# Attention units of four blocks in four PSUM banks, with transposes in steps of their own

## The chip, the cores and the metric

The kernel runs on one core of one Trainium2 chip. The metric is device time in microseconds (us). TensorE is called PE here, VectorE DVE, ScalarE ACT, GpSimd POOL and SyncE SP, as in the profile.

## The reference

Two layers over x of 1 x 1024 x 1024 in float32, each `x <- x + RMSNorm(mixer(RMSNorm(x)))`. Layer 0 is a gated MLP over chunks of 128 tokens; the change doesn't touch it. Layer 1 is attention, 16 heads of 64, in three groups g with (window, dilation) of (128, 1), (512, 4) and (2048, 16), each with q, k and v of its own:

```python
scores = jnp.einsum('brnihk,brnjhk->brnhij', qb, kk) * scale      # a block of 128 queries, its own keys and the block before
scores = jnp.where(valid, scores, -jnp.inf)                       # causal, at most `steps` back
lse = jax.nn.logsumexp(scores, axis=-1)
o = jnp.einsum('brnhij,brnjhk->brnihk', jnp.exp(scores - lse[..., None]), vv)
...
alpha = jax.nn.softmax(jnp.stack(lses, axis=0), axis=0)           # over the three groups
y = jnp.einsum('gbsh,gbshk->bshk', alpha, jnp.stack(outs, axis=0)) * jax.nn.silu(z)
return y @ w_out
```

## The kernel before

Layer 0 takes the first 735 us or so of the span. What follows is layer 1, and the change lies there.

**Projections.** The normalised rows stand transposed in SBUF, each value as a high and a low part, and a product is three matmuls (`mm3`, L82 to L84: high by high, low by high, high by low). Columns of the weights are cut into 40 chunks: for each q (four heads) and each g one chunk of values (`v_chunk`) and two of queries and keys (`qk_chunk`, pair pr = 0 and 1, two heads each), and one of gates for each q (`z_chunk`). A chunk is seven products (`Chunk.run`, Strassen's scheme), in three banks of PSUM with the tag "mm", and a product is four yields of one `mm3`. `pipeline` strings the products together. What a product leaves is added on DVE (`add`, L87) or copied on ACT, in tiles "u" of `newb`. Queries and keys are rotated on DVE and brought into the tiles Q and K of `qk_tile` by 16 DMAs from SP's queue (L705, L706). POOL and DVE form sums of weights and the low parts (L90), ACT the high parts (L96).

**Attention between them.** `drive` walks over the yields of the pipeline. Each yield is a tick; credit grows by RATE, and whenever it reaches one, `step_side` makes one step of attention, which so lands between two projection matmuls. PE's instructions stay in the order in which the program was written (`manual_schedule`); on the other engines and the queues the planner chooses it, and `high_priority(SOON)` moves what it encloses ahead. `done` of a qk chunk puts the attention of its pair into the queue `side`, to start WAIT = 16 ticks later at the earliest.

A `Unit` holds two heads (hh) and two blocks of 128 queries, or four where g is 2 (`lone`: 128 tokens in each of eight residues, with no block before). `scores` computes into two banks "s", one for each head; DVE adds the mask and takes the row's extreme (L773), ACT takes exp and the sum (L776). `transp` turns the weights by PE into two banks "t" (L798), and ACT copies them to PT (L800). `values` multiplies by V in the one bank "o" (L814); ACT copies it to oT (L819), and SP stores oT in DRAM, in od (L820). `attend` makes one step of three units at once: the transposes of the last, the values of the last but one, and the scores of the new one. `TURN` holds the transposes of V (`turned`, L673).

**Merging.** When the three groups of a pair are through, `merge` is put into `slow`, and `step_slow` makes one of its steps every four ticks: it loads the sums (mg), forms the weights of the three groups, turns them (wT), stores them (wd), and for each half of the tokens loads three results from od (mo, L893 to L897) and their weights (mw, L899), multiplies and adds on DVE, and stores in ybd. The last q's merges and the output product follow the pipeline (`fill`, `ending`).

Of the kernel before, what the change touches and what calls it, by code (L numbers as in the profile page):

```python
# [10 lines left out]
F32 = mybir.dt.float32  # L11
# [11 lines left out]
HD = 64  # L23
RATE = 0.125
WAIT = 16
# [8 lines left out]
def trunk_kernel(  # L34
# [613 lines left out]
    def newb(n):  # L648
        return bp.tile([P, 512], F32, tag="u", bufs=9, name=f"b_{n}")

# [84 lines left out]
    class Unit:  # L735
# [16 lines left out]
        def prev(self, b):  # L752
            return (self.g == 0 and b > 0) or (self.g == 1 and b % 2 == 1)

        def scores(self):

            Qt, Kt = QK[self.q, self.g, self.pr]
            pss = [psum("s", [P, 512], f"s_{self.nm}_{hh}") for hh in range(2)]
            for j, use in enumerate(self.use):
                b, cs = self.b + j, slice(use[0] * P, use[-1] * P + P)  # L760
                for hh in range(2):
                    hs_ = slice(64 * hh, 64 * hh + 64)
                    q_ = block(Qt[hs_, :], self.g, b)
                    k_ = block(Kt[hs_, :], self.g, b, len(use) - 1)
                    nc.tensor.matmul(out=pss[hh][:, cs].rearrange("p (n l) -> p n l", l=k_.shape[2]), lhsT=q_, rhs=k_, start=True, stop=True)  # L765
            self.S = [bp.tile([P, 512], F32, tag="St", bufs=2, name=f"St_{self.nm}_{hh}") for hh in range(2)]
            with tc.high_priority(SOON):
                for j, use in enumerate(self.use):
                    cs = slice(use[0] * P, use[-1] * P + P)
                    mk = mask2 if self.lone else mask[:, use[0] % 2 * P:256]  # L770
                    for hh in range(2):
                        m, z = (self.st[:, self.b + j, hh, i:i + 1] for i in range(2))
                        nc.vector.tensor_tensor_reduce(  # L773
                            out=self.S[hh][:, cs], in0=pss[hh][:, cs], in1=mk, scale=-0.125, scalar=3.0e38,
                            op0=ALU.add, op1=ALU.min, accum_out=m)
# [16 lines left out]
        def transp(self):  # L792
            self.PT = bp.tile([P, 2, 4, P], F32, tag="PT", bufs=2, name=f"PT_{self.nm}")
            pT = [psum("t", [P, 4, P], f"pT_{self.nm}_{hh}") for hh in range(2)]
            for hh in range(2):
                for use in self.use:
                    for k in use:
                        nc.tensor.transpose(out=pT[hh][:, k, :], in_=self.S[hh][:, k * P:k * P + P], identity=ident)  # L798
                with tc.high_priority(SOON):
                    nc.scalar.copy(out=self.PT[:, hh, self.first:], in_=pT[hh][:, self.first:])  # L800

        def values(self):

            V, w = VS[self.q, self.g, self.pr], self.n * P
            po = psum("o", [P, w], f"po_{self.nm}")
            if self.lone:
                todo = [(self.b + j, j, 1, j * P) for j in range(4)]
            else:
                todo = [(self.b, 1, 2, 0), (self.b + 1, 3, 1, P)]
                if self.first == 0:  # L810
                    todo.insert(0, (self.b - 1, 0, 1, 0))
            for n, (kb, k, m, o) in enumerate(todo):
                for hh in range(2):
                    nc.tensor.matmul(  # L814
                        out=po[64 * hh:64 * hh + 64, o:o + m * P], lhsT=V[:, kb, hh, :], rhs=self.PT[:, hh, k:k + m, :].rearrange("p k i -> p (k i)"),
                        start=n == 0, stop=n == len(todo) - 1, skip_group_check=True)
            oT = bp.tile([P, 512], F32, tag="oT", bufs=1, name=f"oT_{self.nm}")[:, 0:w]
            with tc.high_priority(SOON):
                nc.scalar.copy(out=oT, in_=po)  # L819
            nc.sync.dma_start(out=od[self.q][self.pr][self.g][:, self.b * P:self.b * P + w], in_=oT)  # L820
# [139 lines left out]
    def step_side(force=False):  # L960

        while side:
            at, work = side[0]
            if at > now[0] and not force:
                return False
            if isinstance(work, Unit):
                side.popleft()
                attend(work)
                return True
            if callable(work):  # L970
# [3 lines left out]
            try:  # L974
                next(work)
                return True
            except StopIteration:
                side.popleft()
        if (force or rate[0] != RATE) and any(going):
            attend(None)  # L980
            return True
        return False

# [195 lines left out]
```

## Time and profile before

| | |
|---|---|
| time, median of 3 runs | 1912.34 us (1910.25 to 1913.97) |
| the profiled execution | 1916.06 us, its span 1914.3 us |
| mean granted clock of TensorE | 0.987 |
| busy: PE, DVE, ACT, POOL | 96%, 68%, 52%, 25% of the span |
| DMA | 242.22 MB, 16 engines used at 43.4% |

The span runs from the first to the last instruction. A row of instructions gives the start, the duration, the engine and line, the tile written and the tiles read, the shape and, in brackets, the idle time before it and what ended it. Matmuls overlap, so that what one costs is read from one start to the next. PEld is PE's loading of weights, SPq the queue of DMA issues on SP.

### The profile page before, as it was taken

Reading aid. Unit: us, or ns where it says so; the run is one execution under the profiler, and the core shown is the slowest. Engines: PE = TensorE matmul, PEld = TensorE weight load, DVE = VectorE, ACT = ScalarE, POOL = GpSimd, SP = SyncE. Lnnn points to the kernel's source line nnn. Section 1 sums busy time; section 2 is a strip of 40 time slices with the busy share of each in tenths; the row PEclk is TensorE's granted clock in tenths of the full one; section 3 lists DMA queues with packets and bytes.
Section 4 is the critical chain, followed back from the end, with each engine's and each line's share of the span. In section 5 each row is a group of like instructions: output and inputs, shape, how many; then the busy total and the mean of one; then the engine's idle time right before and its main releaser. Section 6 shows DMA issues by size and latency. Waiting matters only on the chain.

```text
span 1914.3 us, 29722 instructions
## 1 busy us (share of the span) xinstructions
PE 1836.5 (96%) x10024; PEld 1507.9 (79%) x10024; DVE 1302.0 (68%) x2530; ACT 1002.8 (52%) x2280; POOL 486.1 (25%) x359
## 2 busy tenths in 40 slices
PE   6899999999999897999999999999999999999998
PEld 6899888888888675777778777788777787778777
DVE  6855766576555877558587685669684866868583
ACT  6544455555644665355554457464556444555931
POOL 3331343443300204222213123321233221222100
PEclk9999999999999999999999999999999998999999
DMA  6242433433256575232233554334644335433873
GB/s 209 87 129 82 140 123 114 138 118 96 78 186 232 164 248 183 67 84 74 80 82 88 156 146 119 71 86 125 165 107 105 78 90 156 130 85 74 247 208 110
DMA packets 231847, 242.22 MB, mean 127 GB/s; under 512 B 98448, under 2 KB 150288, under 8 KB 231696
## 3 DMA queue, kind: packets, MB, share of 16 engines
q1 hardware_dynamic: 231696, 240.34, 43.4%
q8 instruction: 79, 1.29, 0.3%
q14 instruction: 72, 0.59, 0.1%
HBM read 170.46 MB, written 44.63 MB: 112 GB/s over the span
## 4 chain that ended last, share of the span: by engine, by line
PE 69%; DVE 11%; DMA 7%; issue 4%; ACT 2%; SPq 2%; POOL 1%; DVEq 0%; POOLq 0%; ACTq 0%
PE p_bqk L82 6%; PE p_bqk L83 5%; PE p_bqk L84 5%; PE p_bv L82 4%; PE p_bv L83 3%; PE p_bv L84 3%; PE s L765 3%; PE po L814 3%; PE p_z L82 3%; PE p_z L84 3%; PE p_z L83 2%; PE p_u L82 2%; PE p_u L83 2%; PE p_u L84 2%; PE pT L798 2%
## 5 line engine op out<-in xcount | busy, mean ns | idle before, releaser
L82 PE MATMUL p_bqk<-b_hi,whi_bqk 128*128 128x512 f32 x672 | 269.8, 401 | 1.6 <-ACT b_x_bqk L239 1.5
L83 PE MATMUL p_bqk<-b_lo,whi_bqk 128*128 128x512 f32 x672 | 262.7, 391 | 0.0
L84 PE MATMUL p_bqk<-b_hi,wlo_bqk 128*128 128x512 f32 x672 | 262.6, 391 | 0.0
L776 ACT ACTIVATE St<-St,st 128x128 f32<-128x128 f32 (+1 forms) x384 | 168.4, 440 | 157.5 <-DVE st L773 155.4
L82 PEld LDWEIGHTS p_bqk<-b_hi,whi_bqk 128*128 128x128 f32 x672 | 126.9, 189 | 41.9 <-issue 10.8
L82 PE MATMUL p_bv<-b_hi,whi_bv 128*128 128x512 f32 x336 | 138.3, 412 | 11.2 <-DVE vt L87 10.0
L84 PEld LDWEIGHTS p_bqk<-b_hi,wlo_bqk 128*128 128x128 f32 x672 | 126.6, 188 | 27.0
L83 PEld LDWEIGHTS p_bqk<-b_lo,whi_bqk 128*128 128x128 f32 x672 | 126.9, 189 | 24.4
L84 PE MATMUL p_bv<-b_hi,wlo_bv 128*128 128x512 f32 x336 | 134.5, 400 | 0.0
L83 PE MATMUL p_bv<-b_lo,whi_bv 128*128 128x512 f32 x336 | 134.4, 400 | 0.0
L773 DVE CUSTOM_DVE_ANT_0 St<-s,mask 128x128 f32<-128x128 f32 (+1 forms) x384 | 110.6, 348 | 31.8 <-PE s L765 31.7
L83 PE MATMUL p_v<-wlo_v,a_hi 128*128 128x256 f32 x448 | 128.3, 287 | 3.9 <-DVE wlo_v L90 3.9
L84 PE MATMUL p_v<-whi_v,a_lo 128*128 128x256 f32 x448 | 128.2, 287 | 3.6 <-DVE sqa L367 2.2
L82 PE MATMUL p_v<-whi_v,a_hi 128*128 128x256 f32 x448 | 128.5, 287 | 2.9 <-DVE v_s_v L87 2.2
L90 POOL TENSOR_TENSOR wt_bqk<-wb_bqk,wt_bqk 128x512 f32<-128x512 f32 x48 | 73.7, 1536 | 193.0 <-DMA wb_bqk<-in_wb_dram 152.9
L90 DVE TENSOR_TENSOR wlo_bqk<-wb_bqk,whi_bqk 128x512 fp32r<-128x512 f32 x96 | 78.9, 822 | 57.0 <-ACT whi_bqk L96 56.3
L96 ACT CAST whi_bqk<-wb_bqk 128x512 fp32r<-128x512 f32 x96 | 59.4, 619 | 110.7 <-PE p_bqk L83 66.0
L84 PE MATMUL po<-oh,yl 128*128 128x512 f32 x256 | 100.7, 398 | 3.5 <-DVE yl L90 3.5
L83 PE MATMUL po<-ol,yh 128*128 128x512 f32 x256 | 100.6, 396 | 1.2 <-DVE ol L90 1.2
L82 PE MATMUL po<-oh,yh 128*128 128x512 f32 x256 | 101.4, 397 | 0.4 <-ACT yh L96 0.4
L90 POOL TENSOR_TENSOR wt_bqk<-wb_bqk,wb_bqk 128x512 f32<-128x512 f32 x24 | 35.1, 1463 | 249.0 <-DMA wb_bqk<-in_wb_dram 170.4
L765 PE MATMUL s<-K,Q 64*128 64x128 f32 (+1 forms) x768 | 87.5, 347 | 7.1 <-DMA K<-b_c 4.7
(262 smaller groups left out, 4820.2 us busy)
## 6 DMA issues: line engine op xcount, KB each, us to landing
wb_bqk<-in_wb_dram SPq DMA_DIRECT2D x96, 256.0 KB, 3.5
wr<-in_woa_dram SPq DMA_DIRECT2D x80, 256.0 KB, 3.6
yr<-yad SPq DMA_DIRECT2D x48, 256.0 KB, 3.4
wb_bv<-in_wb_dram SPq DMA_DIRECT2D x48, 256.0 KB, 3.1
Q<-b_c SPq DMA_DIRECT2D x192, 64.0 KB, 2.2
K<-b_c SPq DMA_DIRECT2D x192, 64.0 KB, 2.1
mo<-od SPq DMA_DIRECT2D x36, 256.0 KB, 3.6
mw<-wd SPq DMA_DIRECT2D x72, 128.0 KB, 3.5
```

What stands on the lines that cost most here:

```text
L82: nc.tensor.matmul(out=pso, lhsT=l_hi, rhs=r_hi, start=start, stop=False, skip_group_check=chained)
L83: nc.tensor.matmul(out=pso, lhsT=l_hi, rhs=r_lo, start=False, stop=False, skip_group_check=chained)
L84: nc.tensor.matmul(out=pso, lhsT=l_lo, rhs=r_hi, start=False, stop=stop, skip_group_check=chained)
L90: (eng or nc.vector).tensor_tensor(out=out, in0=a, in1=b, op=ALU.subtract)
L96: nc.scalar.copy(out=hi, in_=src)
L765: nc.tensor.matmul(out=pss[hh][:, cs].rearrange("p (n l) -> p n l", l=k_.shape[2]), lhsT=q_, rhs=k_, start=True, stop=True)
L773: nc.vector.tensor_tensor_reduce(out=self.S[hh][:, cs], in0=pss[hh][:, cs], in1=mk, scale=-0.125, scalar=3.0e38, op0=ALU.add, op1=ALU.min, ...
L776: nc.scalar.activation(out=self.S[hh][:, cs], in_=self.S[hh][:, cs], func=AF.Exp, scale=-1.0, bias=m, accum_out=z)
L798: nc.tensor.transpose(out=pT[hh][:, k, :], in_=self.S[hh][:, k * P:k * P + P], identity=ident)
L814: nc.tensor.matmul(out=po[64 * hh:64 * hh + 64, o:o + m * P], lhsT=V[:, kb, hh, :], rhs=self.PT[:, hh, k:k + m, :].rearrange("p k i -> p ( ...
```

## The change

A unit has four blocks for each g, so that an attention has two units in place of four where g is 0 or 1. Scores of blocks 0 and 1 stand in the banks "s", those of blocks 2 and 3 in the banks "t", one bank for each head and half, and the transposes use the same four banks afterwards. PT becomes a tile for each head. A step is either the values of the unit before together with the scores of the new one, or the transposes of the unit alone; after the first the credit falls by 1.3, after the second by 0.7. The credit goes no higher than one and falls only for a step that was made. RATE goes from 0.125 to 0.145. Of "u" there are eight buffers in place of nine, of mw one in place of two, and the copy of wT gets the higher priority.

```diff
-RATE = 0.125
+RATE = 0.145
+EXPS = 1.3
...
-        return bp.tile([P, 512], F32, tag="u", bufs=9, name=f"b_{n}")
+        return bp.tile([P, 512], F32, tag="u", bufs=8, name=f"b_{n}")
...
-            self.n = 4 if self.g == 2 else 2
-            self.b, self.last = self.n * u, self.n * u + self.n == 8
+            self.b, self.last = 4 * u, u == 1
...
-                self.use = [[2 * j + kk for kk in range(0 if self.prev(self.b + j) else 1, 2)] for j in range(2)]
-            self.first = self.use[0][0]
+                self.use = [[2 * j + kk for kk in range(0 if self.prev(self.b + j) else 1, 2)] for j in range(4)]
+            slots = [k for use in self.use for k in use]
+            self.halves = [[k for k in slots if k // 4 == half] for half in range(1 if self.lone else 2)]
...
+        def banks(self, name):
+            return [[psum("st"[half], [P, 512], f"{name}_{self.nm}_{hh}_{half}") for half in range(len(self.halves))] for hh in range(2)]
+
         def scores(self):
...
-            pss = [psum("s", [P, 512], f"s_{self.nm}_{hh}") for hh in range(2)]
+            pss = self.banks("s")
...
-            self.S = [bp.tile([P, 512], F32, tag="St", bufs=2, name=f"St_{self.nm}_{hh}") for hh in range(2)]
+            self.S = [bp.tile([P, 1024], F32, tag="St", bufs=2, name=f"St_{self.nm}_{hh}") for hh in range(2)]
...
         def transp(self):
-            self.PT = bp.tile([P, 2, 4, P], F32, tag="PT", bufs=2, name=f"PT_{self.nm}")
-            pT = [psum("t", [P, 4, P], f"pT_{self.nm}_{hh}") for hh in range(2)]
-            for hh in range(2):
-                for use in self.use:
-                    for k in use:
-                        nc.tensor.transpose(out=pT[hh][:, k, :], in_=self.S[hh][:, k * P:k * P + P], identity=ident)
-                with tc.high_priority(SOON):
-                    nc.scalar.copy(out=self.PT[:, hh, self.first:], in_=pT[hh][:, self.first:])
+            self.PT = [bp.tile([P, 8, P], F32, tag="PT", bufs=2, name=f"PT_{self.nm}_{hh}") for hh in range(2)]
+            pT = self.banks("pT")
+            for half, slots in enumerate(self.halves):
+                for hh in range(2):
+                    for k in slots:
+                        nc.tensor.transpose(out=pT[hh][half][:, k % 4 * P:k % 4 * P + P], in_=self.S[hh][:, k * P:k * P + P], identity=ident)
+                    with tc.high_priority(SOON):
+                        nc.scalar.copy(out=self.PT[hh][:, slots[0]:slots[-1] + 1, :].rearrange("p k i -> p (k i)"), in_=pT[hh][half][:, slots[0] % 4 * P:slots[-1] % 4 * P + P])
...
-                todo = [(self.b, 1, 2, 0), (self.b + 1, 3, 1, P)]
-                if self.first == 0:
-                    todo.insert(0, (self.b - 1, 0, 1, 0))
+                todo = [(self.b - 1, 0, 1, 0)] if self.use[0][0] == 0 else []
+                todo += [(self.b + j, 2 * j + 1, 2 if j < 3 and self.prev(self.b + j + 1) else 1, j * P) for j in range(4)]
...
+        def steps(self):
+            settle()
+            self.scores()
+            going.append(self)
+            yield EXPS
+            self.transp()
+            yield 2.0 - EXPS
+
+    going = deque()
+
+    def settle():
+        if going:
+            going.popleft().values()
+
     def attention(q, g, pr):
         st = bp.tile([P, 8, 2, 2], F32, tag="st", bufs=2, name=f"st_{q}_{g}_{pr}")
-        units = [Unit((q, g, pr, st), u) for u in range(2 if g == 2 else 4)]
-
-        return units[:2] + [TURN.pop((q, g))] + units[2:] if pr == 0 else units
-
-    going = [None, None]
-
-    def attend(unit):
-
-        if going[0]:
-            going[0].transp()
-        if going[1]:
-            going[1].values()
-        if unit:
-            unit.scores()
-        going[:] = [unit, going[0]]
+        units = [Unit((q, g, pr, st), u).steps() for u in range(2)]
+
+        return [units[0], TURN.pop((q, g)), units[1]] if pr == 0 else units
...
-        nc.scalar.copy(out=wT, in_=wt_[0:48, :])
+        with tc.high_priority(SOON):
+            nc.scalar.copy(out=wT, in_=wt_[0:48, :])
...
-            w = bp.tile([P, 512], F32, tag="mw", bufs=2, name=f"mw_{nm}_{th}_{g}")
+            w = bp.tile([P, 512], F32, tag="mw", bufs=1, name=f"mw_{nm}_{th}_{g}")
...
             try:
-                next(work)
-                return True
+                return next(work) or 1.0
             except StopIteration:
                 side.popleft()
-        if (force or rate[0] != RATE) and any(going):
-            attend(None)
-            return True
-        return False
+        if (force or rate[0] != RATE) and going:
+            settle()
+            return 1.0
+        return 0.0
...
-            credit[0] = min(credit[0] + rate[0], 2.0)
+            credit[0] = min(credit[0] + rate[0], 1.0)
             if credit[0] >= 1.0:
-                credit[0] -= 1.0
-                step_side()
+                credit[0] -= step_side()
```

## Rows read from the trace of the kernel before

**Rows 1.** The page's busy times: share of the span, instructions.

```profile
PE 1836.5 (96%) x10024; PEld 1507.9 (79%) x10024; DVE 1302.0 (68%) x2530; ACT 1002.8 (52%) x2280; POOL 486.1 (25%) x359
```

**Rows 2.** Stretches: us, busy (count) of PE, PEld, DVE, ACT, POOL, clock, DMA.

```profile
800.00:1830.00 1030.00, 1005.50 (x5624) 799.32 (x5623) 730.29 (x1613) 564.52 (x1516) 246.74 (x160) 0.99 0.43 114
...
1260.00:1262.00 2.00, 2.00 (x15) 1.79 (x14) 1.41 (x3) 2.00 (x9) 0.00 (x0) 1.00 0.00 0
...
1617.20:1627.40 10.20, 8.04 (x28) 5.42 (x25) 4.62 (x12) 4.89 (x15) 2.08 (x2) 0.50 0.61 149
```

**Rows 3.** Timeline of PE: one attention step (g = 2) between projection matmuls.

```profile
1272.18 0.39 PE L84 MATMUL p_bqk<-b_hi,wlo_bqk 128*128 128x512 f32 x1
1272.41 1.03 PE L798 MATMUL pT<-ident,St 128*128 128x128 f32 x8
1273.38 1.09 PE L814 MATMUL po<-PT,V 128*64 128x128 f32 x16
1274.40 1.16 PE L765 MATMUL s<-K,Q 64*128 64x128 f32 x16
1275.49 0.50 PE L82 MATMUL p_bv<-b_hi,whi_bv 128*128 128x512 f32 x1
1275.83 0.40 PE L83 MATMUL p_bv<-b_lo,whi_bv 128*128 128x512 f32 x1
```

**Rows 4.** Timeline of PE: eight transposes of V between projection matmuls.

```profile
1260.61 1.05 PE L673 MATMUL pvt<-ident,vt 128*128 128x128 f32 x8
...
1261.73 0.39 PE L83 MATMUL p_bv<-b_lo,whi_bv 128*128 128x512 f32 x1
```

**Rows 5.** List of waits, 800 to 1830 us: total us, times, longest.

```profile
ACT St L776 <- DVE st L773: 155.4, 68, 7.7
...
ACT oT L819 <- DMA od<-oT: 14.4, 6, 3.8
...
PE p_bv L82 <- DVE vt L87: 10.0, 4, 3.0
...
PE s L765 <- DMA K<-b_c: 4.7, 7, 0.9
...
PE pT L798 <- ACT St L776: 3.5, 6, 1.7
```

**Rows 6.** Timeline of PE: two projections' ends; first scores of (1, 2, 0).

```profile
1230.77 0.39 PE L84 MATMUL p_bqk<-b_hi,wlo_bqk 128*128 128x512 f32 x1
...
1241.88 0.82 PE L798 MATMUL pT<-ident,St 128*128 128x128 f32 x6
...
1245.53 1.13 PE L765 MATMUL s<-K,Q 64*128 64x128 f32 x14 [0.88 <-DMA K<-b_c]
...
1567.87 0.40 PE L84 MATMUL p_bqk<-b_hi,wlo_bqk 128*128 128x512 f32 x1
```

**Rows 7.** Timeline of SP: issues of Q, K for three pairs, first and last.

```profile
1231.35 0.69 SPq L705 DMA_DIRECT2D Q<-b_c  x1
...
1243.15 0.61 SPq L706 DMA_DIRECT2D K<-b_c  x1
...
1567.54 0.56 SPq L705 DMA_DIRECT2D Q<-b_c  x1
...
1578.09 0.59 SPq L706 DMA_DIRECT2D K<-b_c  x1
...
1590.75 1.72 SPq L705 DMA_DIRECT2D Q<-b_c  x1
...
1615.23 0.59 SPq L706 DMA_DIRECT2D K<-b_c  x1
```

**Rows 8.** The page's DMA issues: count, KB each, us to landing.

```profile
mw<-wd SPq DMA_DIRECT2D x72, 128.0 KB, 3.5
```

**Rows 9.** Groups of ACT by form: busy us, mean ns | idle before.

```profile
L776 ACT ACTIVATE St<-St,st 128x256 f32<-128x256 f32 x176 | 87.3, 497 | 71.3 <-DVE st L773 71.2
...
L800 ACT COPY PT<-pT 128x512 f32<-128x512 f32 x80 | 42.9, 591 | 1.6 <-PE pT L798 1.5
```

More of the change, by code (lines that the diff above doesn't have):

```diff
@@ L748, in __init__ @@
             else:
-                self.use = [[2 * j + kk for kk in range(0 if self.prev(self.b + j) else 1, 2)] for j in range(2)]
-            self.first = self.use[0][0]
+                self.use = [[2 * j + kk for kk in range(0 if self.prev(self.b + j) else 1, 2)] for j in range(4)]
+            slots = [k for use in self.use for k in use]
+            self.halves = [[k for k in slots if k // 4 == half] for half in range(1 if self.lone else 2)]
         def prev(self, b):
             return (self.g == 0 and b > 0) or (self.g == 1 and b % 2 == 1)
+        def banks(self, name):
+            return [[psum("st"[half], [P, 512], f"{name}_{self.nm}_{hh}_{half}") for half in range(len(self.halves))] for hh in range(2)]
         def scores(self):
             Qt, Kt = QK[self.q, self.g, self.pr]
-            pss = [psum("s", [P, 512], f"s_{self.nm}_{hh}") for hh in range(2)]
+            pss = self.banks("s")
             for j, use in enumerate(self.use):
-                b, cs = self.b + j, slice(use[0] * P, use[-1] * P + P)
+                b, half, at = self.b + j, use[0] // 4, use[0] % 4 * P
                 for hh in range(2):
@@ L764, in scores @@
                     k_ = block(Kt[hs_, :], self.g, b, len(use) - 1)
-                    nc.tensor.matmul(out=pss[hh][:, cs].rearrange("p (n l) -> p n l", l=k_.shape[2]), lhsT=q_, rhs=k_, start=True, stop=True)
-            self.S = [bp.tile([P, 512], F32, tag="St", bufs=2, name=f"St_{self.nm}_{hh}") for hh in range(2)]
+                    o_ = pss[hh][half][:, at:at + len(use) * P]
+                    nc.tensor.matmul(out=o_.rearrange("p (n l) -> p n l", l=k_.shape[2]), lhsT=q_, rhs=k_, start=True, stop=True)
+            self.S = [bp.tile([P, 1024], F32, tag="St", bufs=2, name=f"St_{self.nm}_{hh}") for hh in range(2)]
             with tc.high_priority(SOON):
                 for j, use in enumerate(self.use):
+                    half, at = use[0] // 4, use[0] % 4 * P
                     cs = slice(use[0] * P, use[-1] * P + P)
@@ L773, in scores @@
                         nc.vector.tensor_tensor_reduce(
-                            out=self.S[hh][:, cs], in0=pss[hh][:, cs], in1=mk, scale=-0.125, scalar=3.0e38,
+                            out=self.S[hh][:, cs], in0=pss[hh][half][:, at:at + len(use) * P], in1=mk, scale=-0.125, scalar=3.0e38,
                             op0=ALU.add, op1=ALU.min, accum_out=m)
@@ L792, in transp @@
         def transp(self):
-            self.PT = bp.tile([P, 2, 4, P], F32, tag="PT", bufs=2, name=f"PT_{self.nm}")
-            pT = [psum("t", [P, 4, P], f"pT_{self.nm}_{hh}") for hh in range(2)]
-            for hh in range(2):
-                for use in self.use:
-                    for k in use:
-                        nc.tensor.transpose(out=pT[hh][:, k, :], in_=self.S[hh][:, k * P:k * P + P], identity=ident)
-                with tc.high_priority(SOON):
-                    nc.scalar.copy(out=self.PT[:, hh, self.first:], in_=pT[hh][:, self.first:])
+            self.PT = [bp.tile([P, 8, P], F32, tag="PT", bufs=2, name=f"PT_{self.nm}_{hh}") for hh in range(2)]
[6 more added lines that the diff above has]
+                        nc.scalar.copy(out=self.PT[hh][:, slots[0]:slots[-1] + 1, :].rearrange("p k i -> p (k i)"), in_=pT[hh][half][:, slots[0] % 4 * P:slots[-1] % 4 * P + P])
         def values(self):
-            V, w = VS[self.q, self.g, self.pr], self.n * P
-            po = psum("o", [P, w], f"po_{self.nm}")
+            V = VS[self.q, self.g, self.pr]
+            po = psum("o", [P, 512], f"po_{self.nm}")
             if self.lone:
@@ L814, in values @@
                     nc.tensor.matmul(
-                        out=po[64 * hh:64 * hh + 64, o:o + m * P], lhsT=V[:, kb, hh, :], rhs=self.PT[:, hh, k:k + m, :].rearrange("p k i -> p (k i)"),
+                        out=po[64 * hh:64 * hh + 64, o:o + m * P], lhsT=V[:, kb, hh, :], rhs=self.PT[hh][:, k:k + m, :].rearrange("p k i -> p (k i)"),
                         start=n == 0, stop=n == len(todo) - 1, skip_group_check=True)
-            oT = bp.tile([P, 512], F32, tag="oT", bufs=1, name=f"oT_{self.nm}")[:, 0:w]
+            oT = bp.tile([P, 512], F32, tag="oT", bufs=1, name=f"oT_{self.nm}")
             with tc.high_priority(SOON):
                 nc.scalar.copy(out=oT, in_=po)
-            nc.sync.dma_start(out=od[self.q][self.pr][self.g][:, self.b * P:self.b * P + w], in_=oT)
+            nc.sync.dma_start(out=od[self.q][self.pr][self.g][:, self.b * P:self.b * P + 512], in_=oT)
             if self.last:
@@ L964, in step_side @@
             if at > now[0] and not force:
-                return False
-            if isinstance(work, Unit):
-                side.popleft()
-                attend(work)
-                return True
+                return 0.0
             if callable(work):
@@ L974, in step_side @@
             try:
-                next(work)
-                return True
+                return next(work) or 1.0
             except StopIteration:
                 side.popleft()
-        if (force or rate[0] != RATE) and any(going):
-            attend(None)
-            return True
-        return False
+        if (force or rate[0] != RATE) and going:
+            settle()
+            return 1.0
+        return 0.0
     def step_slow():
```

## The prediction

> **What bounds the kernel now.** I read the busy shares first: the matrix engine (PE) is busy 96% of the span [rows 1], so what counts is the work on PE and the gaps between its instructions. Then the table by stretches: the attention stage, from 800 to 1830 us of the span, holds 1005.5 us of PE work in 1030 us, at a mean granted clock of 0.99 [rows 2]. At most some 25 us of gaps and about 10 us of clock (1% of 1030) can be won there; everything else must come out of PE's own work. PE runs in the order in which the program was written, so each attention step stands as a block inside the stream of projection matmuls. The timeline of one such block shows its make-up: eight transposes, 16 value matmuls, 16 score matmuls, and back to the projections [rows 3]. The reader should look at starts, not at durations (matmuls overlap): projections start 0.23 us apart, and the first one after the block is followed by the second only after 0.34 us.
>
> **The work of PE.** Scores and transposes stay the same in number. What falls is the number of blocks that hold values and scores: per (q, g, pair) four units become two where g is 0 or 1, so 80 become 48; 48 blocks of transposes alone are new. What does a block cost beyond its matmuls? Eight transposes alone take 1261.73 - 1260.61 = 1.12 us up to the second projection, less one 0.23 us pitch: 0.89 us, or 0.11 each [rows 4]. Before values they take 1273.38 - 1272.41 = 0.97 us [rows 3], so the turn to the values costs 0.08. The way back from scores to projections costs 0.34 - 0.23 = 0.11 [rows 3]. The turn from values to scores can't be seen by itself; it lies between nothing and the 0.11 of the way back, and I take 0.10, since the other two turns are near that. That is 0.29 us for a set of three turns, and 80 - 48 = 32 sets fewer: -9.3 us (-6 with nothing for the middle one; -13 if each of the three costs 0.13). I assume that going from a projection to values costs what going from a transpose does; if it cost nothing, another 4 us would be won. The 48 blocks of transposes alone add nothing, since eight alone cost 0.89 = 8 x 0.11.
>
> Where g is 0 a unit of two blocks needs an extra matmul for the key block shared with its neighbour. In the trace's records (an f32 matmul is two), one pair of heads has 28 narrow and 16 wide ones before, 12 and 24 after. Sixteen narrow ones take 1.02 us [rows 3]; eight wide ones cost between half of that (no cost for width) and all of it (twice the cost). So 0 to 0.5 us is won in each of eight: 0 to 4, and I take 2. **PE work: -11 us**, between -6 and -21.
>
> **When scores start.** Q and K reach their tiles by 16 DMAs after the projection has ended. Counting through the driver's rule (a step about every eight ticks of three projection matmuls before; as soon as the credit allows after), the first scores of the twelve first pairs came 16 ticks after their projection seven times and 20 ticks five times. After, all twelve come at exactly 16, the twelve second pairs at 23 (20 to 32 before, 19 for the last). The list of waits has the scores waiting on K seven times, 4.7 us [rows 5], as many as there are starts at 16. One of them in detail: the projection ends at 1231.16, PE has done its 16 ticks at 1241.88, that is 10.7 us later, and the scores stop for K until 1245.53, 14.4 us after the end [rows 6]; the last of the 16 issues begins 12.0 us after the end [rows 7]. Transposes and values stood ahead of the scores and hid some 1.8 us of it. After, only values stand there, about 1.1 us, so that scores are due at 11.8 and this start waits 2.5 us. That is for g = 2. For g = 0, the start of (3, 0, 0): the projection ends at 1568.27 [rows 6], the last issue begins at 1578.09 [rows 7], 9.8 us later; landing in the same time as the other, K is there at 12.2 and the scores wait 0.4. For g = 1 I take the middle, 1.4. Four of each: 17 us, against today's 4.7. **Waits for K: +12 us**, between nothing (all as at g = 0) and +25 (all as at g = 2).
>
> **The collisions around merges.** Merges of earlier heads (q, pair) put their loads on the same SyncE queue. There ScalarE waited six times, 14.4 us in all, to overwrite oT, whose store to od was still queued [rows 5]; its exps stood behind, so the transposes waited (3.5 us), VectorE's sums came late, and the projections waited on vt, 10.0 us in four places [rows 5]. After the last of these the clock was granted at half, 1.2 GHz, for 10 us [rows 2]. The change copies a whole 512-wide oT every 14 ticks in place of half of one every eight, so its store has nearly twice the time. Of 13.5 us of waits and some 10 us of clock I let half go: **-12 us**, between 0 and -23.
>
> Against that, mw has one buffer in place of two: each load of weights lands 3.5 us after its issue [rows 8], and now waits for the last product. A merge with six such loads gets up to three landings, some 10 us, longer, and what is queued behind a waiting load on SyncE are Q and K, od stores and projection weights. Today a merge spreads the 16 issues of the pair (3, 0, 1) from 1590.75 to 1615.23, that is 24.5 us [rows 7], 14 more than without one; its scores came at 32 ticks and didn't wait. After they come at 23: 22 us with three blocks in between, against some 27 until K lands. I put +4 us in the sum: about that at one of the three places, the rest hidden by merges that begin some eight ticks sooner.
>
> **Edits at nothing.** Half as many oT copies and od stores for g = 0 and 1 (32 fewer), hidden because neither queue sets PE's pace. The ninth buffer u: with eight, the x1 copy of the next projection would need one only after the Q and K DMAs of the last one have read theirs; two projection products hide that, and it costs ScalarE a microsecond or two where Q and K are late. The copy of wT at higher priority: ahead of work that PE waits for less. Copies of four banks of transposes before the next scores: five ticks, 3.4 us, cover four copies of 0.59 [rows 9]; without that cover each copy that is late holds the next scores for as long.
>
> **Exps.** In the 32 units with g 0 or 1 eight exps of 256, 497 ns each [rows 9], stand in place of four, and nine ticks (6.1 us) lie before the transposes in place of eight. The eight need about 4.5 us behind the first, which leaves 1.6 us plus what starts during the scores. VectorE kept ScalarE waiting 155.4 / 68 = 2.3 us on average when it waited at all [rows 5]. I count 0; if each of 32 waited 0.7 us it would be +22.
>
> **Sum.** -11 + 12 - 12 + 4 = -7 us. On the profiled execution, 1916.06 (a span of 1914.3 and what lies around it), this gives 1909; that execution is 3.7 us above the median of the runs, 1912.34, so on the runs it is 1905.
>
> **Rivals.**
> *Slower: Q and K late behind merges.* Merges now begin about eight ticks sooner, while the first pair of the next q loads its Q and K, and that pair starts at 16 ticks without cover. If half of the 14 us falls on it, PE stands 7 us at three starts and about as long at the three g-1 starts behind the second merge: +20 to +40. With -11 and +12, and the collisions gone by half or kept, this ends at 1921 to 1953; the likeliest of it is around 1932. For it speak rows 7, against it that the store of oT no longer queues as often. It decides from about 4 us at each of six starts.
> *No change: the waits eat it.* -11 and +12 as above, but the collisions stay as they are and one buffer of mw costs what the spared stores save: 1909 to 1916.
> *Slower: exps late*, as above: 1920 to 1930. Against it: transposes wait only 3.5 us in all today [rows 5].
> *Slower: the clock.* In this trace transposes alone, eight at a time, ran at the full 2.4 GHz, granted 1.00 [rows 2]. The blocks are up to twice as long after, and stand alone. If all 560 of them in the stage went at half, 1.2 GHz, each would cost its 0.11 us once more: 62 us, 1967. The Trainium skill (TensorE: Matmul & The Clock Gate, Part 4) says that a transpose doesn't count as activity for the clock the way a matmul does, which would make this case the one to expect. The trace doesn't agree as far as it goes: its eight alone went at 1.00.
>
> **How the numbers follow.** Forecast 0.45 (its own range 1889 to 1909); waits eat it 0.24; late Q and K 0.23; late exps 0.05; clock 0.03. 0.2% is 3.8 us, about what a measurement of this kernel can tell from no change. Faster: 0.42 of the forecast and 0.02 of the second case, so 0.44; same: 0.03 and 0.18, so 0.21; slower: 0.04 of the second and the last three cases, 0.31 together, so 0.35. The range 1887 to 1936 leaves out the deepest gains (all collisions gone and every bound good) and the far end of late Q and K, with the clock.
>
> **What would show it.** 48 blocks with values straight after a projection matmul, starts 1.0 us before the scores; PE's value matmuls down from 864 to some 800 records; scores waiting on K about twelve times and 17 us; the wait of oT on od nearly gone and p_bv on vt well below 10 us. The prediction is wrong if scores wait on K by 5 us and more at a place, if the transposes' wait on St is above 10 us, or if granted clock below 1 covers more than the stage's 1%.

## The result and the profile after

The changed kernel takes 1936.91 us (median of 4 runs, 1936.20 to 1942.28); the kernel before, beside it on the same chip, 1913.15 us (4 runs). The ratio is 1.0138, with a 95% interval of 1.0122 to 1.0154: slower by 24 us between the medians (26 by the ratio), where 1905 us was forecast. The profiled execution took 1936.20 us (a span of 1934.5), 20 us more than that of before.

The page's busy times after, to be read against [rows 1]:

```profile
PE 1832.5 (95%) x9960; PEld 1514.0 (78%) x9960; DVE 1287.6 (67%) x2530; ACT 997.6 (52%) x2248; POOL 477.9 (25%) x359
```

PE has 64 instructions and 4 us of busy time fewer in a span that is 20 us longer. So the loss is idle time, or work at the lower clock. Three stretches after, as in [rows 2] (the eighth column of numbers is the granted clock):

```profile
842.00:844.30 2.30, 2.30 (x20) 2.13 (x19) 0.90 (x2) 1.46 (x4) 0.00 (x0) 1.00 0.53 113
800.00:1850.00 1050.00, 1000.22 (x5562) 803.01 (x5561) 716.57 (x1619) 562.33 (x1487) 238.37 (x160) 0.98 0.43 112
1327.00:1333.80 6.80, 5.05 (x19) 3.76 (x20) 4.94 (x14) 1.86 (x8) 1.15 (x1) 0.50 0.40 121
```

The attention stage is 20 us longer with 5 us less PE work in it, 50 us idle where there were 25, and its clock fell from 0.99 to 0.98. The stretches at 0.50 add up to 44 us in it after, to 24 before. The list of waits after, against [rows 5]:

```profile
DVE mo L94 <- DMA mw<-wd: 40.7, 9, 6.3
PE s L770 <- DMA K<-b_c: 26.5, 15, 6.1
PE p_bz L83 <- ACT b_x_bz L240: 6.9, 2, 5.9
PE pT L804 <- DVE st L779: 5.4, 6, 1.4
PE s L770 <- issue: 5.0, 6, 2.0
PE pT L804 <- DVE mo L88: 2.6, 6, 0.4
```

The waits of oT on od and of p_bv on vt are gone. In their place the scores wait on K: 26.5 us in 15 places, up to 6.1 us in one (4.7 us before), and 5.0 more put down to issue. VectorE's wait for mw in the first line was 0.4 us before. The worst three are the first scores of (1,0,0), (2,0,0) and (3,0,0). PE's timeline at (2,0,0): the last projection matmul of its Q and K, the last one ahead of the block, the block.

```profile
1309.57 0.39 PE L85 MATMUL p_bqk<-b_hi,wlo_bqk 128*128 128x512 f32 x1
...
1321.25 0.39 PE L85 MATMUL p_bqk<-b_hi,wlo_bqk 128*128 128x512 f32 x1
1321.57 1.09 PE L819 MATMUL po<-PT,V 128*64 128x128 f32 x16
1328.24 0.76 PE L770 MATMUL s<-K,Q 64*128 64x128 f32 x2 [5.57 <-DMA K<-b_c]
1329.51 2.08 PE L770 MATMUL s<-K,Q 64*128 64x128 f32 x9 [0.51 <-issue]
```

PE has done its 16 ticks 11.7 us after the projection (1321.25 - 1309.57), and then stands for K, nearly 7 us counting the halt behind the first two scores. As PE stands the clock goes to half: it is granted at 0.50 from 1327.0 to 1333.8 (above). SyncE's issues in that time (start, duration) show what was late:

```profile
1308.95 1.15 SPq L907 DMA_DIRECT2D mw<-wd  x2
1312.36 0.57 SPq L706 DMA_DIRECT2D Q<-b_c  x1
...
1315.39 1.12 SPq L907 DMA_DIRECT2D mw<-wd  x2
...
1319.09 0.59 SPq L707 DMA_DIRECT2D K<-b_c  x1
...
1320.56 0.60 SPq L905 DMA_DIRECT2D mo<-od  x1
1321.75 1.11 SPq L907 DMA_DIRECT2D mw<-wd  x2
1322.92 0.58 SPq L706 DMA_DIRECT2D Q<-b_c  x1
...
1327.35 0.59 SPq L707 DMA_DIRECT2D K<-b_c  x1
```

The same pair in the kernel before, whose Q and K projection ended at 1304.45:

```profile
1303.72 0.56 SPq L705 DMA_DIRECT2D Q<-b_c  x1
...
1315.29 0.59 SPq L706 DMA_DIRECT2D K<-b_c  x1
1315.92 3.15 SPq L899 DMA_DIRECT2D mw<-wd  x4
```

Before, the merge's loads of mw stand right behind the last K; after, one pair of them stands ahead of the first Q and two among Q and K. The first comes 1.0 us ahead of the projection's end (1309.96), where it was 11.5 us behind it. The last K goes out 17.4 us after the projection's end, where it was 10.8. VectorE has its part, since its products of the merge stand ahead of those that make Q and K:

```profile
1307.43 0.19 DVE L870 TENSOR_TENSOR e<-mg 128x16 f32<-128x16 f32 x1 [3.44 <-DMA mg<-sd]
...
1310.42 0.68 DVE L94 TENSOR_TENSOR b_c<-p_bqk,cos_t 128x512 f32<-128x512 f32 x1
...
1318.26 0.69 DVE L91 TENSOR_TENSOR b_c<-b_c,b_x_bqk 128x512 f32<-128x512 f32 x1
...
1319.46 1.07 DVE L94 TENSOR_TENSOR mw<-mo,mw 128x512 f32<-128x512 f32 x1
...
1321.04 0.69 DVE L88 TENSOR_TENSOR mo<-mo,mw 128x512 f32<-128x512 f32 x1
```

It stands 3.44 us for the merge's mg and begins the first product of Q and K at 1310.42, so that the first Q goes out 2.4 us after the projection's end, where it was 0.7 us ahead of it. The second half of Q and K is ready with the sum that ends at 1318.95, but its first issue comes at 1322.92: on the queue ahead of it the load of mo goes out as the merge's product ends (1320.53), and the load of mw as its sum ends (1321.73), which reads the only buffer. So of the 6.6 us that the last K is later, 3.1 are there at the first Q, by VectorE; the other 3.4 or so come in the queue, about 1.3 within the first half and 2.0 ahead of the second.

**The sums.** Taking for each matmul the distance from the start of the one ahead of it, less the usual distance of two such kinds (the 20th percentile over the traces), the stream from the first projection of layer 1 to the last is about 22 us longer after (it begins 2 us sooner). The scores account for +29, transposes +10, the last projections (p_bz) +10, those of Q and K +3, p_bv -11, and the rest, about -18, is less work. What half clock costs is contained in these, and each is good to a microsecond or two. Of the scores' +29, 25 are at the three starts (1,0,0), (2,0,0) and (3,0,0).

**PE's work** shows in two places. The records of values went from 608 narrow and 256 wide (864) to these 800, the number foreseen:

```profile
L819 PE MATMUL po<-PT,V 128*64 128x256 f32 x320 | 43.9, 387 | 0.0
L819 PE MATMUL po<-PT,V 128*64 128x128 f32 x480 | 39.7, 278 | 0.0
```

And the blocks for g = 1: one of before (first fence), the two kinds after (second).

```profile
920.98 0.39 PE L84 MATMUL p_bv<-b_hi,wlo_bv 128*128 128x512 f32 x1
921.21 0.82 PE L798 MATMUL pT<-ident,St 128*128 128x128 f32 x6
...
924.19 0.39 PE L84 MATMUL p_bqk<-b_hi,wlo_bqk 128*128 128x512 f32 x1
```

```profile
902.66 0.39 PE L85 MATMUL p_bqk<-b_hi,wlo_bqk 128*128 128x512 f32 x1
902.89 1.47 PE L804 MATMUL pT<-ident,St 128*128 128x128 f32 x12
...
904.65 0.39 PE L85 MATMUL p_bqk<-b_hi,wlo_bqk 128*128 128x512 f32 x1
...
913.17 0.39 PE L85 MATMUL p_bv<-b_hi,wlo_bv 128*128 128x512 f32 x1
913.49 1.52 PE L819 MATMUL po<-PT,V 128*64 128x256 f32 x16
...
917.02 0.40 PE L85 MATMUL p_bv<-b_hi,wlo_bv 128*128 128x512 f32 x1
```

Each from the start of the projection matmul ahead to that of the third behind, less three pitches of 0.23: 2.52 us before; 1.30 and 3.16 after. Two blocks of before, 5.04, became 4.46: 0.58 for one set of turns spared, twice the 0.29 assumed. Two such units in each of eight pairs of heads spare 9 us; the blocks for g = 0, taken the same way, spare another 9 (about 12.0 us of blocks in one pair before, 10.9 after); for g = 2 it is 3.20 before and 0.88 + 2.32 after, nothing. Together about 18 us.

**The tail** lost 10 us. PE stands 6 us for a copy on ScalarE:

```profile
1826.30 0.79 PE L83 MATMUL p_bz<-b_hi,whi_bz 128*128 128x512 f32 x1 [5.89 <-ACT b_x_bz L240]
```

```profile
1819.71 1.28 ACT L782 ACT_TABLE_LOAD   x1 [0.67 <-DVE st L779]
1821.00 0.40 ACT L782 ACTIVATE St<-St,st 128x128 f32<-128x128 f32 x1
...
1825.67 0.58 ACT L240 COPY b_x_bz<-p_bz 128x512 f32<-128x512 f32 x1
```

The copy's place on ScalarE is behind a table load and the eight exps of a unit. By the sums p_bz takes 7 to 11 us more in every run of the changed kernel here than in the kernel before, whatever its merges do.

### The profile page after: what moved, and what is told of

Its sections match the earlier page's. It is cut to its first block, busy times and chain, and to the rows that moved or that the text cites. A ratio compares the mean times of both kernels' runs of the same rounds, so it can differ in the third digit from the quotient of the medians.

```text
span 1934.5 us, 29476 instructions
## 1 busy us (share of the span) xinstructions
PE 1832.5 (95%) x9960; PEld 1514.0 (78%) x9960; DVE 1287.6 (67%) x2530; ACT 997.6 (52%) x2248; POOL 477.9 (25%) x359
## 4 chain that ended last, share of the span: by engine, by line
PE 63%; DVE 13%; DMA 10%; SPq 3%; issue 3%; ACT 2%; POOL 1%; DVEq 0%; POOLq 0%; ACTq 0%
DMA mw<-wd 4%; PE p_bqk L83 4%; PE p_bqk L85 4%; PE p_bqk L84 4%; PE p_bv L83 3%; PE p_bv L84 3%; PE p_bv L85 3%; PE s L770 3%; PE p_z L83 2%; PE p_z L84 2%; PE p_z L85 2%; PE p_u L83 2%; PE p_u L84 2%; PE p_u L85 2%; PE pT L804 2%
## 5 line engine op out<-in xcount | busy, mean ns | idle before, releaser
L91 POOL TENSOR_TENSOR wt_bqk<-wb_bqk,wt_bqk 128x512 f32<-128x512 f32 x48 | 69.2, 1442 | 209.2 <-DMA wb_bqk<-in_wb_dram 126.7
L770 PE MATMUL s<-K,Q 64*128 64x128 f32 (+1 forms) x768 | 85.5, 350 | 31.5 <-DMA K<-b_c 26.5
L770 PEld LDWEIGHTS s<-K,Q 64*128 64x128 f32 x768 | 63.8, 196 | 45.2 <-issue 37.6
```

The lines of the kernel that those rows point to most:

```text
L91: (eng or nc.vector).tensor_tensor(out=out, in0=a, in1=b, op=ALU.subtract)
L770: nc.tensor.matmul(out=o_.rearrange("p (n l) -> p n l", l=k_.shape[2]), lhsT=q_, rhs=k_, start=True, stop=True)
```

## The experiments

Ratios are to the kernel before, run beside each on the same chip; its median was 1907.21 us for the first four, 1910.95 for the next four, 1911.19 and 1911.99 for the last two pairs. The theory: Q and K come late because merges now load while a pair that starts without cover waits for them. The rivals: 16 ticks are too few with or without merges; the single mw buffer; and, for the end alone, the rate of the last steps. RATE itself, the eighth u and the priority of wT's copy were not undone alone.

**Later starts.** The changed kernel, with the last q's g = 2 left at 16:

```diff
-            later(lambda: attention(q, g, pr), WAIT)
+            later(lambda: attention(q, g, pr), 16 if (q, g) == (3, 2) else 20)
```

and the same with 26 and 29 in place of 20.

> The changed kernel, with the attention of a pair starting 20 ticks after its projection in place of 16 (the last pairs, q = 3 and g = 2, stay at 16, so that the end is as it was). Theory (scores due before K is there): every first pair gets four ticks, 2.7 us, more; the small waits of some 1 to 2 us vanish, the three of about 6.5 us behind merges fall to some 4, so the scores' wait on K goes from 26.5 to about 11 us and the time from 1937 to about 1915. Rival (deeper units: eight exps and four copies in one go hold PE): the waits on St and PT stay, the time stays within 5 us of 1937. Rival (one buffer of mw stretches merges and blocks the queue): K comes as late after the projection as before, and where it comes later than 20 ticks the wait stays; this does not tell it from the theory.

> As the run with 20 ticks, with 26 ticks, 6.8 us more than the changed kernel. Theory: all waits on K at first pairs but the last q's third group vanish (26.5 to about 3 us), with them most of the half clock that follows them (44 us of it in the attention stage of the changed kernel, some 20 us without), and the time falls to about 1895, below the kernel before. Rival (deeper units): within 5 us of 1937. If moving the start only moves the collision with the merges to another place, between 1910 and 1930, with new waits of PE on St or on V.

> The changed kernel with 29 ticks of wait in place of 26 (16 kept at the last q, g = 2). If cover of Q and K were still short at 26, 2 to 5 us less than 26 gave; if 26 covers all of them, within 0.2% of its 0.993, since the same work only lies three ticks later.

With 20 ticks: 1918.14 us, 1.0061 [1.0042, 1.0080]. With 26: 1894.94 us, **0.9933 [0.9910, 0.9956]**, which beats the kernel before. With 29: 1919.12 us, 1.0031 [1.0015, 1.0047]. The waits with 20 ticks, where projections of Q and K also stand 22.8 us for a copy on ScalarE, and (second fence) with 26, where the scores have only 0.6 us left:

```profile
PE s L770 <- DMA K<-b_c: 12.0, 7, 3.1
```

```profile
PE s L770 <- DMA K<-b_c: 0.6, 1, 0.6
```

Ten ticks, some 7 us, are worth about 39 us by the ratios. By the sums above (the profiled execution with 26 ticks was 6 us under its median, and its stream is 46 us shorter) 38 come from the scores and 13 from the transposes, and 14 are given back in projections of Q and K; the stretches at half clock fall from 44 to 20 us. At (1,0,0), (2,0,0) and (3,0,0) the last K goes out 10 to 11 us after the projection again, since the merges move back with the attention steps: at (2,0,0) the first load of mw now comes 13.6 us behind the projection's end. K is late at (q,0,1) (23 to 24 us) and (q,1,0) (18 to 22) in their place, which start at 33 and 26 ticks. But 29 isn't better still, as either theory had it; now VectorE is late for V:

```profile
PE p_bv L83 <- DVE vt L88: 20.8, 9, 5.5
```

By the sums p_bv loses 30 us against the run with 26, all of the difference between the two streams (28). Later starts push the steps onto other work, so 26 is a place between two collisions, not a rule. Why VectorE is late for V with 29 and not with 26 was not followed further.

**Later starts at six places only.**

```diff
+            later(lambda: attention(q, g, pr), 26 if g < 2 and q > 0 else WAIT)
```

> The changed kernel with the wait of 26 ticks only at the heads of g = 0 and g = 1 of q = 1 to 3, the six starts that lie under a merge; the other six first pairs keep 16. Theory (Q and K late under merges at six starts): nearly the whole gain of 26 ticks everywhere comes, a ratio of 0.995 to 1.000 to the kernel before; the scores' wait on K is below 8 us, at the g = 2 starts and those of q = 0 alone, 1 to 2 us each. Rival (K is late by its own chain at all twelve starts, as my sum had it at 1.4 us each): half of the gain, a ratio of 1.003 to 1.008.

1914.30 us, 1.0013 [1.0000, 1.0027]: between the two expectations. The six starts under merges give back about 24 us of the loss (1.0138 to 1.0013), the five others some 15 more. By the sums the scores' part of the loss is gone with the six alone (-31 us, of which 20 go again in projections of Q and K); with the five others it falls by 7 more, the transposes by 8 and the projections by 7. So K's own chain at 16 ticks does cost something, but at these five starts the scores lose within 1 us of what they lose in the kernel before: it isn't what the change added. Since the later starts move the merges too, the run doesn't tell their two effects apart.

**Merges eight ticks later**, two empty steps at the head of each:

```diff
     def merge(q, pr, last=False):
...
+        if not last:
+            yield
+            yield
```

> The changed kernel, with each merge beginning eight ticks later (two empty steps at its start), where its loads stood against the next projections before the change. Theory (merge loads queued among the Q and K transfers make the three long waits): the waits of 5.6 to 6.2 us at the first pairs of q = 1, 2, 3 shrink to the 1 us of the others, the time falls by 20 to 30 us, to about 1910. Rival (K is late at 16 ticks whatever the merges do): the three waits stay above 4 us, the time stays within 8 us of 1937.

1935.04 us, 1.0152 [1.0133, 1.0172]: no gain, against the theory's 20 to 30 us.

```profile
PE s L770 <- DMA K<-b_c: 32.4, 13, 8.5
```

K was in time at the g = 0 starts (10 to 12 us from the projection's end to the last issue, and some 1 us of PE standing at most), as the theory had it, but 22 to 24 us at (1,1,0), (2,1,0) and (3,1,0), each with 8 to 9 us of PE standing. The collision moved with the merge, from one start at 16 ticks to the next.

**The merges emptied**, in the changed kernel and in the one before. Each half of a merge of q = 0 to 2 only carries one od half to ybd:

```diff
-            ow0, ow1 = load(th, 0), load(th, 1)
-            yield
...
-            add(acc, acc, weighted(2, ow2))
+            acc = bp.tile([P, 512], F32, tag="mo", bufs=2, name=f"mo_{nm}_{th}_0")
+            nc.sync.dma_start(out=acc, in_=od[q][pr][0][:, HALVES[th]])
+            yield
+            yield
             nc.sync.dma_start(out=ybd[c][:, HALVES[th]], in_=acc)
```

> The changed kernel, 16 ticks and one mw buffer, with the halves of the merges of q = 0 to 2 emptied: each loads one od half and stores it to ybd as it is; the twelve mw loads, four od loads and the products of such a merge are left out, so that its output is not the reference's. If the merges' loads make Q and K late at starts without cover: the three stalls before (1,0,0), (2,0,0) and (3,0,0) fall from 6.5 us to 2 or less, the chain from the projection's end to the last of the 16 issues is 11 to 13 us at all twelve, and the ratio to the kernel before is 0.990 to 1.000. If 16 ticks are too few by themselves: stalls of 3 us and more stay at many starts, ratio above 1.005.

> The kernel before with the same emptied merges, as the other half of the comparison. If the kernel before pays little for its merges, because the pair that loads under them starts at 32 ticks: 0.2 to 0.8% faster than before (its collisions of oT and vt gone), and the changed kernel with emptied merges is 0 to 0.5% faster than this one, the gain in PE's work less the K waits of the earlier starts. If the change loses by something other than the merges: the changed one with emptied merges is still 0.5% or more slower than this one.

The changed kernel: 1895.19 us, **0.9910 [0.9889, 0.9932]**. The kernel before: 1899.19 us, **0.9929 [0.9911, 0.9947]**. So the merges' halves cost the kernel before about 14 us and the changed one about 44 us; without them the change gives some 4 us, with intervals that overlap, so that even the sign is barely told. The changed one's waits, then those of the kernel before:

```profile
PE s L770 <- DMA K<-b_c: 15.7, 14, 3.5
```

```profile
PE p_bv L82 <- DVE vt L87: 8.4, 4, 2.2
PE s L765 <- DMA K<-b_c: 4.1, 5, 1.2
```

The transposes' share falls by 15 us in the changed kernel, that of the scores by 15, the projections' by 8. The last K goes out 10 to 12 us after the projection at the first pairs where no head of a merge is left; at the three g = 0 starts, where it is, 13.5 to 15.5, with the first Q about as late as in the changed kernel (2.3 to 3.1 us after the end), and some 3 us of standing remain. That fits the split read at (2,0,0): the halves take the time in the queue, the head that on VectorE.

**The single mw buffer**: in the kernel before alone; and undone in the changed one, with seven u in place of eight to make room, at 16 ticks and at 26.

```diff
-            w = bp.tile([P, 512], F32, tag="mw", bufs=2, name=f"mw_{nm}_{th}_{g}")
+            w = bp.tile([P, 512], F32, tag="mw", bufs=1, name=f"mw_{nm}_{th}_{g}")
```

> The kernel before with one mw buffer in place of two, nothing else of the change. If the single buffer by itself delays Q and K by more than their cover (my term of 4 us, and more by the rival): 0.2 to 0.6% slower, scores' wait on K above its 4.7 us, Q and K of the second pair of g = 0 later than 24 us after the projection. If it is nothing: a ratio within 0.2% of 1, and VectorE's wait for mw grows alone.

> The changed kernel, 16 ticks kept, with two mw buffers and seven u in place of one and eight. If the single mw buffer makes Q and K late (the second mw load of a merge stands on the SyncE queue until a product that the merge writes a step later): the stalls of about 6.5 us before the scores of (1,0,0), (2,0,0) and (3,0,0) fall below 2 us, and the ratio to the kernel before falls from 1.014 to 0.992 to 1.002. If it is only the merge's number of loads beside a start without cover: the three stalls stay at 4 us and more, and the ratio at 1.008 to 1.014.

> The changed kernel with 26 ticks of wait, two mw buffers and seven u in place of one and eight. If the single buffer still costs: the stalls of the projections behind late Q and K DMAs (p_bqk on b_x_bqk, wlo_bqk, p_bv on vt, some 8 us with the half clock behind them) shrink and the ratio falls from 0.993 to 0.985 to 0.990. If only the cover counts: within 0.2% of 0.993, or worse where seven u are too few, which shows as waits of x copies on the Q and K DMAs.

One buffer in the kernel before: 1938.09 us, **1.0132 [1.0106, 1.0158]**, as much by itself as the whole change, and more than twice the most that was expected. Two in the changed kernel: 1937.49 us, 1.0137 [1.0116, 1.0158], nothing won. Two with 26 ticks: 1896.37 us, 0.9923 [0.9900, 0.9946], the same as with one. The kernel before with one buffer:

```profile
PE p_bv L82 <- DVE vt L87: 16.4, 4, 5.4
PE s L765 <- DVE wlo_bqk L90: 9.8, 3, 3.4
PE s L765 <- DMA K<-b_c: 4.9, 7, 1.0
```

and one of SyncE's own waits in it, a load of mo behind a merge's product, 6.6 us in the kernel before:

```profile
SPq L897 <- DVE mw L93: 20.4, 5, 4.6
```

Scores of (1,1,0), (2,1,0) and (3,1,0), which start at 16 ticks, come 3 us late (put down to another engine there, the 9.8 us, so not in the K row), and the projections wait on vt. By the sums 9 us are the scores', 10 p_bv's and 6 the last projections'. In the changed kernel two buffers do shorten the three stalls, but only from nearly 7 to some 4.5 us:

```profile
PE s L770 <- DMA K<-b_c: 20.5, 15, 3.4
```

What is won there (10 us of scores by the sums) goes again in projections and transposes. So the single buffer costs 25 us in the kernel before, and giving the second one back wins nothing in the changed kernel, at 16 ticks or at 26. Seven u are part of both of these runs: a gain by the buffer and a loss by the missing u could cancel in them, and no run here separates the two.

**One buffer, loads in the order of use**: a load of weights is issued only behind the product that frees mw.

```diff
-            ow0, ow1 = load(th, 0), load(th, 1)
+            ow0 = load(th, 0)
             yield
             acc = ow0[0]
             mul(acc, acc, ow0[1])
-            ow2 = load(th, 2)
+            ow1 = load(th, 1)
+            yield
             add(acc, acc, weighted(1, ow1))
+            ow2 = load(th, 2)
             yield
```

> The changed kernel, 16 ticks and one mw buffer kept, but each merge loads the weights of the next g only behind the product that frees mw, so that no load is issued long before it can start; each half of a merge takes three loads in a row. If the load that waits on the queue is what delays Q and K: the three stalls fall below 3 us, a ratio of 0.995 to 1.005. If a merge with one buffer is simply longer and meets Q and K anyhow: stalls of 4 us and more stay there or turn up at (1,1,0), (2,1,0) and (3,1,0), 1.008 to 1.016.

1932.66 us, 1.0103 [1.0086, 1.0120]: some 7 us better. The longest stall falls from 6.1 to 3.1 us, and at (q,1,0) K now goes out 18 to 19 us after its projection, with 2 to 3 us of standing there: the places and the ratio are those of the second expectation, the stalls smaller than its 4 us. A load that stands in the queue is part of the delay; by this run, in which a merge's loads also come in three turns in place of two, its part is the smaller one.

**The rate of the last steps**, RATE3 0.25 in place of 0.16.

> The changed kernel, with RATE3 = 0.25 in place of 0.16, so that the last four units are through 17 ticks before the projections end (1086 of 1104 in place of 1103). Theory on the end: the last chunk lost some 10 us to a copy of a gate product that stood behind eight exps and a table load on ScalarE (PE waited 5.9 us, then ran 6.8 us at half clock); with the exps earlier this goes, and the time falls by 5 to 10 us, to about 1929. Rival (the end is held by something else): within 3 us of 1937.

1931.95 us, 1.0136 [1.0117, 1.0154]: no gain. PE's stall in the tail stays:

```profile
1828.44 0.80 PE L83 MATMUL p_bz<-b_hi,whi_bz 128*128 128x512 f32 x1 [7.79 <-ACT b_x_bz L240]
```

The exps lie earlier, but the copy now stands behind a cast that waits 4.5 us for weights of the output projection. That the tail's loss is the eight exps is thus not shown; that it is the copy's place in ScalarE's order is what both traces show.

## Why the prediction was wrong

**The step that failed** is the term for merges: the +4, "about that at one of the three places, the rest hidden by merges that begin some eight ticks sooner". Beginning sooner hid nothing; it brought the merge onto the pair that starts at 16 ticks. The cover of the g = 0 starts had been read at (3,0,0), a wait of 0.4 us, where the merge's mw loads came only behind the last K. After the change the last K went out 17.2 us after the projection there, not 9.8, and these starts stood 6.6 to 7.3 us at q = 1 to 3. Of the scores' +29 us by the sums, 25 are at these three. The sign that the prediction named against itself, a wait of 5 us at one place, is met with 6.1. The term beside it, "Waits for K: +12 us", came out too high for its own reason: the chain at 16 ticks without a merge's start over it added some 5 us at the nine other starts, half of it behind the second merge. With the merges' halves emptied in both kernels the scores still differ by some 19 us, 16 of it at the three g = 0 starts, beside the heads of merges that were left. For Q and K the prediction counted merges on the SyncE queue alone; that their head keeps VectorE from making Q and K, 3.1 us at (2,0,0), was not in it.

**The rival** *Q and K late behind merges* is what happened: its three starts and its price (7 us each), and the 1936.91 us lie in its 1921 to 1953. The merges' halves cost 30 us more than in the kernel before (44 against 14), within its +20 to +40. That the total came so near its likeliest, 1932, is in part luck, since the transposes and the tail below, 10 us each, were in no term of it, and the work fell by 7 us more than it took. Its second half, as much at the g = 1 starts, was too high: 1 to 3 us each there.

**PE's work** was mis-sized in the safe direction: 18 us, not 11, inside the bounds of 6 to 21. A set of three turns costs 0.58 us, not 0.29, since the turns before values and between values and scores, which could not be seen alone, cost more than the 0.08 and 0.10 taken.

**The collisions**: the waits of oT on od and of p_bv on vt went entirely, more than the half assumed. But the clock, of which half of 10 us was to come back, got worse: 44 us at half in the stage, not 24, in stretches that follow PE's standing, as at 1327.0. The condition that the prediction named against itself, granted clock below 1 over more than 1% of the stage, is met with 4%; but it was met before the change too, since 24 us at half are 2.3% of the stage, and a mean of 0.99 is 1% of clock lost, not 1% of the time.

**The exps**: 0 was taken. The list of waits has the transposes waiting 8 us in place of 3.5, and their share by the sums is +10; it vanishes (1 us left against 16) when the merges' halves are emptied. VectorE stood 40.7 us for mw, with the sums of the scores behind it. So the cause isn't the eight exps that the rival named but merges again.

**The clock rival** did not come: sixteen transposes alone, from 842.26, took 1.75 us with the projection's turn behind them, at a granted clock of 1.00 (the first stretch above). The Trainium skill (TensorE: Matmul & The Clock Gate, Part 4) has a transpose not count as a matmul does for the clock. The trace doesn't agree as far as these blocks go, twice as long as those of before.

**The tail's** 10 us were not in the prediction at all: a copy that comes late on ScalarE.

So the 20 us between the profiled executions are: work -18, p_bv -11; scores +29, 25 of it under merges, the transposes +10, the tail +10. The +3 in projections of Q and K and the 2 us by which the stream begins sooner about cancel. On the runs, without the merges' halves the balance is about -4, and with 26 ticks it is -13. Whether the kernel before would gain from later starts as well was not tried; it stays open how much of the 26-tick version's lead is the four-block units' own.

## What to carry to other kernels

A start that is held only by "so many ticks after" has as much cover as the busiest thing that can stand in its queue leaves it. When a change makes steps come sooner or evens out their spacing, list what else moves with them (here the merges, loads and products alike), and lay the new dates of every producer beside the new dates of its consumer, place by place; an average over starts that didn't meet says nothing about ones that will. And taking one of two buffers from loads that share a queue with something urgent is not priced by their own landing time: alone it cost 25 us here in the kernel before, while giving it back to the changed kernel, with a u less, won nothing.

## What the runs showed of the hardware

- Going from transposes to values, on to scores and back to projections, a set of three turns, cost more than could be seen of it: a set that was spared was worth 0.58 us, where 0.08 and 0.11 were visible.
- Sixteen f32 transposes in a row ran at the full clock, 0.10 to 0.11 us each.
- PE standing for some 6 us went along with granted clock 0.50 for 6.8 to 10.2 us, beginning before its work did (1327.0, with scores from 1328.24). Nine records of scores took 2.08 us there, where sixteen took 1.16 in [rows 3]; so a stall of 6 us cost more than 6.
- SyncE's issues of Q and K came 0.63 us apart in an unbroken row (1322.92 to 1327.35, eight of them), so that 16 take some 10 us even with nothing between them, the larger part of the 11 us that 16 ticks give.
- SyncE's queue kept its order: Q and K that were ready at 1318.95 went out at 1322.92, behind loads of mo and mw that stood for VectorE's products.
